# The RG-LRU gate products of a one-layer decoder step in float32r, with their low parts made on GpSimd

## The chip, the cores and the metric

The kernel runs on one core of one Trainium2 chip. A core has five engines that run at the same time, each with its own list of instructions: TensorE (PE in the profile, its weight loads PEld) multiplies matrices and writes to PSUM, VectorE (DVE) and ScalarE (ACT) work on tiles of 128 partitions, GpSimd (POOL) can do simple tile operations but reaches no PSUM, and SyncE (SP) only issues DMAs. An engine executes its list in order; semaphores make it wait for others. The metric is the device time of one execution in microseconds (us). Before the change it is 1437.67 us, the median of three runs (1437.34 to 1437.91).

## The reference

One layer of a decoder for a prompt of 256 tokens and 8 single-token samples, so 264 columns (N) that go through the same weights. The part that the change touches is the recurrent group (RG-LRU) at its beginning:

```python
  xn = rmsnorm(x, g_mix);  z = xn @ w_in
  xr, conv_new = causal_conv(z[..., OFF_RGX:OFF_RGG], conv_buf, conv_w, conv_b)
  r  = sigmoid(block_diag(xr, w_rg_a, b_rg_a))      # 8 blocks of 128 x 128
  ig = sigmoid(block_diag(xr, w_rg_x, b_rg_x))
  log_a = -RG_C * r * softplus(-lam);  a = exp(log_a)
  h  = scan(a, sqrt(1 - exp(2 * log_a)) * (ig * xr), h0)
```

Beside it in the same layer stands an mLSTM group, which also updates a matrix state C for each of the 8 samples and 4 heads, then come the output projection, attention to 256 memory tokens and a SwiGLU network. Everything is float32 in the reference.

## The kernel before

**Three passes.** In this kernel's trace four float32 products of 264 columns take TensorE 1.58 us, while one in float32r, a shorter form, follows the last after 0.11 us. The kernel therefore splits nearly every operand x into a high part h (x copied to float32r, on ScalarE) and a low part x - h (on VectorE), and `mm3` (L287) does three float32r matmuls: high by high, high by low, low by high. The right operand is taken in another column order (`turn`), so a result in PSUM is read back with `unturn` and written with `halves`. The gate products are an exception: `rg_gen` multiplies fp32 by fp32, one matmul for each of 8 chunks and 2 gates.

**Steps.** The weights come in steps of 128 x 2048 elements, listed in `steps`: four steps for the first quarter columns of w_in (0 to 3), four single ones (4 to 7) that finish the eight chunks of the recurrent input, step 8 for the mLSTM gates (`pe_if`), then q and k, v, the recurrent gate branch (from step 25), and so on. The main loop (L1489) goes through them. For step i it first hands out the evacuations of earlier steps, splits the weights of step i + 1 (`split_half`, two halves h0 and h1, with high priority; `st["split"]` and `st["low"]` remember the last high and low part), emits the matmuls of step i, loads the weights of step i + 3 on SP (`load_piece`, five buffers "raw"), and calls `pump`. The split weights lie in four buffers "w", so a half waits until TensorE is through with the one four halves earlier.

**Side work.** `pump` (L323) runs generators such as `rg_gen`, `ml_gates`, `ml_sample` up to a due time, by price formulas for VectorE and ScalarE (L65 to L96); a generator that yields STEP goes on at the next pump at the earliest. What the pump emits has only a place in the program. The tile framework's scheduler then orders the instructions of each engine itself, by priority and by its own simulated times, except on SP and where `in_order` or `manual_schedule` fixes the order of the program: ScalarE and VectorE up to step 3, TensorE up to step 6. `tc.issue_after(x)` puts an instruction behind x on x's engine.

**The first steps.** In steps 0 to 3 a piece of w_in holds four chunks, `load_first` (L209) sends each of the first six chunks (4 i + c < 6) as a DMA of its own, and the others two by two. SP's list (L1463 to L1475) takes turns between parts of x and chunks; behind piece 1 it sends `vecs[:, 16:]`, all vectors of the layer but the first gain.

**Recurrence.** `evac_rgx` brings a chunk from PSUM into a tile, `rg_conv` makes the convolution on VectorE, and `rg_gen` (started at step 7) loads the gate weights (`wrg`, two DMAs of 512 KB on SP), makes the coefficients (`rg_coef`), and after every second chunk emits four gate products and their sigmoids. The tiles come from the pool "B" with 26 buffers.

**Samples.** `ml_sample` (L859) goes through 4 heads and 8 samples: two ScalarE copies with a scale into t2, one VectorE update of C, two VectorE products with a sum; C goes out by DMA from GpSimd's queue.

Of the kernel before, what the change touches and what calls it, by code (L numbers as in the profile page):

```python
# [17 lines left out]
P = 128  # L18
# [77 lines left out]
def layer_kernel(ctx: ExitStack, tc, xT, memT, vec, wrg, w_in, w_out, w_q, w_k, w_v, w_o,  # L96
# [112 lines left out]
    def load_first(i, c):  # L209

        src = steps[i][0].rearrange("p (n c m) -> p n c m", c=4, m=P)
        if c % 2 == 0:
            raws.setdefault(i, []).append(B([P, 1024]))
        r = raws[i][c // 2].rearrange("p (n c m) -> p n c m", c=2, m=P)
        if 4 * i + c < 6:
            sp.dma_start(r[:, :, c % 2], src[:, :, c])
        elif c % 2:
            sp.dma_start(r, src[:, :, c - 1: c + 1])
# [307 lines left out]
                                 ts[:, :, 0:1], op0=OP.mult, op1=OP.add)  # L526

    def rg_gen():
        wr = [B([P, 8, P]), B([P, 8, P])]
        for j in range(2):  # L530
            sp.dma_start(wr[j], wrg[:, j * 8: j * 8 + 8, :])
        rg_coef()
        r, ig = Arr(RGB), Arr(RGB)
        for n in range(RGB):
            while rg["zn"] <= n:
                yield STEP
            rg_conv(n)
            yield 1.5
            if n % 2 == 0:
                continue  # L540
            yield STEP
            for q in (n - 1, n):
                for t, j, b in ((r, 0, "ba"), (ig, 1, "bx")):
                    ps = bank("ax")
                    pe.matmul(ps[:, :N], wr[j][:, q, :], rg["xr"](q), start=True, stop=True)
                    last = act.activation(t(q), ps[:, :N], AF.Sigmoid, bias=V(b, q))
            yield 0.1
        yield STEP
        xr, c = rg["xr"], rg["c"]
        e2 = Arr(RGB)  # L550

        for n in range(RGB):
            with tc.issue_after(last.ins), tc.issue_after(st["split"].ins):
                act.activation(e2(n), r(n), AF.Exp, scale=c[:, 8 + n: 9 + n])
                le = act.activation(r(n), r(n), AF.Exp, scale=c[:, n: n + 1])
                act.activation(e2(n), e2(n), AF.Relu, scale=-1.0, bias=ones[:, 0:1])
            dve.tensor_mul(ig(n), ig(n), xr(n))
            yield 0.8
        for n in range(RGB):
            with tc.issue_after(le.ins), tc.issue_after(st["split"].ins):  # L560
                act.activation(e2(n), e2(n), AF.Sqrt)
            dve.tensor_mul(ig(n), ig(n), e2(n))
            yield 0.4
        h = Arr(RGB)
        rg["h"] = h
        for n in range(RGB):
            dve.tensor_tensor_scan(h(n)[:, :T], r(n)[:, :T], ig(n)[:, :T], 0.0, op0=OP.mult, op1=OP.add)
            yield 0.6
        h0 = V("h0", 0, 64).rearrange("p (n b) -> p n b", b=NS)
        for q in range(2):  # L570
            hq, rq_, iq = (t.tile(q)[:, :, T:N] for t in (h, r, ig))
            dve.tensor_mul(hq, rq_, h0[:, 4 * q: 4 * q + 4, :])
            dve.tensor_add(hq, hq, iq)
            act.activation(hlast[:, 4 * q: 4 * q + 4, :], h.tile(q)[:, :, T - 1: N], AF.Copy)
        yield 0.3
# [52 lines left out]
    def evac_if(ps):  # L628
        R = Arr(7)
        ml["R"] = R  # L630
        for q in range(2):
            pool_e.memset(R.tile(q), 0.0)
        x, a = R(0)[0:36], R(1)[0:36]
        act.activation(gbias[0:4], V("bi")[0:4], AF.Copy)
        act.activation(gbias[32:36], V("bf")[0:4], AF.Copy)
        act.activation(halves(a), unturn(ps[64:100, :N]), AF.Copy)
        dve.tensor_add(halves(x), unturn(ps[0:36, :N]), halves(a))
        dve.tensor_mul(x, x, rstd[0:36, :])
        dve.tensor_scalar(x, x, gbias[0:36], None, op0=OP.add)
        ml["gates"] = side(ml_gates(), 0)  # L640
# [218 lines left out]
    def ml_sample():  # L859
        while not ml["gates"].done:  # L860
            yield STEP
        qk = ml["qk"]
        ks, qs = qk.tile(1)[:, :, T:N], qk.tile(0)[:, :, T:N]
        sc, Dg = bcs[:, :, 0:8], bcs[:, :, 8:16]

        def load(h, b4):
            C = B([P, 4, 2, P])
            pool_e.dma_start(C, c0T[h, :, b4 * 4: b4 * 4 + 4])
            return C

        loaded = [load(0, 0), load(0, 1)]
        x = ltmp(64)
        kd = ltmp(32).rearrange("p (h b) -> p h b", b=NS)
        by4 = lambda t: t.rearrange("p h (g b) -> p h g b", b=4)
        x4 = x.rearrange("p (h g j b) -> p h g j b", g=2, j=2, b=4)
        dve.tensor_mul(kd, ks, Dg)
        dve.tensor_copy(x4[:, :, :, 0], by4(kd))
        dve.tensor_copy(x4[:, :, :, 1], by4(qs))
        n0 = V("n0", 0, 32).rearrange("p (h b) -> p h b", b=NS)
        dve.tensor_mul(snew, n0, sc)  # L880
        dve.tensor_add(snew, snew, kd)
        dve.tensor_mul(ssum[:, 1], snew, qs)
        yield 0.6
        yield STEP
        ps = bank("ax")
        pe.transpose(ps[0:64, 128:256], x, ident)
        yield STEP
        rows = ltmp(128)
        act.activation(rows[0:64, :], ps[0:64, 128:256], AF.Copy)
        scr = drm.tile([64, P], F32, name="scr")  # L890
        pool_e.dma_start(scr, rows[0:64, :])
        yield 0.5
        def fetch(h, b4):
            C = loaded.pop(0) if loaded else load(h, b4)
            kq = B([P, 2, 4, P])
            r0 = (2 * h + b4) * NS
            src = scr[r0: r0 + NS, :].rearrange("b d -> (b d)")
            ml["fetch"] = pool_e.dma_start(kq.rearrange("p j b d -> p (j b d)"), src.partition_broadcast(P))
            return C, kq

        ahead = [fetch(0, 0), fetch(0, 1)]
        yield STEP
        for h in range(H):
            while ml.get("vn", 0) < 2 * h + 2 or "last" not in ml:
                yield STEP
            for b4 in range(2):
                C, kq = ahead.pop(0)
                n = 2 * h + b4 + 2
                for bb in range(4):
                    b = b4 * 4 + bb  # L910
                    t2 = sb.tile([P, 264], F32, tag="dw", bufs=2, name=nm("dw"))[:, 0: T]
                    t2 = t2.rearrange("p (v d) -> p v d", d=P)
                    with tc.issue_after(ml["exp"].ins):
                        for vb in range(2):
                            act.activation(t2[:, vb, :], kq[:, 0, bb, :], AF.Copy,
                                           scale=ml["v"](2 * h + vb)[:, T + b: T + b + 1])
                    with tc.issue_after(ml["last"].ins):
                        dve.scalar_tensor_tensor(C[:, bb], C[:, bb], sc[:, h, b: b + 1], t2,
                                                 op0=OP.mult, op1=OP.add)
                    j = sb.tile([P, 2, T], F32R, tag="ds", bufs=2, name=nm("ds"))[:, 0, 0: P].bitcast(F32)  # L920
                    for vb in range(2):
                        dve.scalar_tensor_tensor(j, C[:, bb, vb, :], 1.0, kq[:, 1, bb, :], op0=OP.mult,
                                                 op1=OP.mult, accum_out=nums[:, 2 * h + vb, b: b + 1])
                    yield 0.8
                if n < 2 * H:
                    ahead.append(fetch(n // 2, n % 2))
                with tc.issue_after(ml["fetch"].ins):
                    last = pool_e.dma_start(o_sc[h, :, b4 * 4: b4 * 4 + 4], C)
        while min(ml.get("pn", 0), ml.get("vtn", 0)) < H:
            yield STEP  # L930
        with tc.issue_after(last.ins):
            pool_e.dma_start(kept_k, ml["kb"])
            for q in range(2):
                ml["kept"] = pool_e.dma_start(kept_v[q], ml["vts"][q])
            pool_e.dma_start(o_h, hlast)
            pool_e.dma_start(o_cp, cpo)
            pool_e.dma_start(o_cs, cso)
            pool_e.dma_start(o_sn, snew)
        yield 0.1
# [529 lines left out]
    for i in range(1, 3):  # L1469
        for c in range(0, 4, 2):  # L1470
            load_x(sp, 4 * i + c, 4 * i + c + 2)
            load_first(i, c)
            load_first(i, c + 1)
        if i == 1:
            sp.dma_start(vecs[:, 16:], vec[:, 16:])  # L1475
    kept, early = ExitStack(), ExitStack()
    kept.enter_context(tc.manual_schedule(engines={mybir.EngineType.PE}))
    early.enter_context(in_order())
# [10 lines left out]
    for i, (src, cols, pef, evf, need) in enumerate(steps):  # L1489
# [41 lines left out]
        if i == 0:  # L1531
            for c in range(0, 4, 2):
                load_x(sp, 12 + c, 14 + c)
                load_first(3, c)
                load_first(3, c + 1)
        else:
            load_piece(i + LD)
        pump(pe.clock + SLACK)
        if i == 24:
            st["ng"] = side(ml_norm(), 6)  # L1540
# [122 lines left out]
```

## Time and profile before

| what | value |
|---|---|
| time, median of 3 runs | 1437.67 us |
| the profiled execution's own time | 1437.94 us |
| its span, first to last instruction | 1436.2 us |
| mean granted TensorE clock | 0.998 |
| PE ax<-B,B 128x264, the gate products | 32 records, mean 389 ns |
| PE mm<-B,w 128x264, float32r | 10448 records, mean 276 ns |
| DVE w<-raw,w 128x1024, a low part | 488, mean 1232 ns |
| ACT w<-raw 128x1024, a high part | 488, mean 1056 ns |
| POOL subtractions 128x256 | 32 in L1213 (mean 1143 ns), 16 in L1267 (mean 996 ns) |

A record's duration on TensorE is from its entry into the array to its modelled end; records overlap, so what a matmul costs is the distance from one start to the next. A timeline row reads: start, duration, engine, line, operation, output<-inputs, size, count, and in brackets the idle time before it with what ended it. A row of windows holds for each engine its busy time and count (PE, PEld, DVE, ACT, POOL), then the granted clock, the share of the DMA engines and GB/s. L61 is the line of a helper through which all PE, DVE and ACT instructions go, so groups are told apart by tiles.

### The profile page before, as it was taken

What the parts mean: (1) busy time and instruction counts of PE and PEld (TensorE: products, weight loads), DVE (VectorE), ACT (ScalarE), POOL (GpSimd) and SP (SyncE); (2) the same over time, 40 slices, a digit from 0 to 9 for tenths busy, and PEclk for the clock granted to TensorE, in tenths of its full rate; (3) what the DMA queues carried; (4) which work ended last, traced back from release to release, by engine and by line L of the source; (5) the groups of instructions that cost most, each with busy time, mean ns of one, the idle gap of its engine ahead of it and who ended that gap; (6) DMA issues with size and microseconds to landing.
All of it is one profiled execution on the core that took longest, in us unless ns stands there. A gap on an engine that the chain in (4) does not pass through costs nothing.

```text
span 1436.2 us, 29864 instructions
## 1 busy us (share of the span) xinstructions
PE 1423.6 (99%) x11959; PEld 1401.9 (98%) x11959; DVE 1039.2 (72%) x1974; ACT 802.7 (56%) x1291; POOL 125.1 (9%) x195
## 2 busy tenths in 40 slices
PE   9999999999999999999999999999999999999997
PEld 9999999999998999999999999999999999999997
DVE  7957898997899999977666655555656655566565
ACT  7778876775556666665554444334444433444474
POOL 0000220000224434300000000000000000000000
PEclk9999999999999999999999999999999999999999
DMA  8755897557899887846555555555555555555573
GB/s 301 232 195 179 303 360 294 186 194 252 289 347 388 295 335 273 322 161 214 192 192 200 195 192 200 197 191 195 201 192 193 200 195 192 198 196 194 164 242 127
DMA packets 98139, 329.16 MB, mean 229 GB/s; under 512 B 10864, under 2 KB 17440, under 8 KB 98000
## 3 DMA queue, kind: packets, MB, share of 16 engines
q1 hardware_dynamic: 81840, 271.96, 54.1%
q0 software_dynamic: 15296, 54.21, 10.2%
q8 instruction: 93, 1.52, 0.4%
q10 hardware_dynamic: 864, 1.08, 0.2%
q14 instruction: 46, 0.38, 0.1%
HBM read 314.36 MB, written 12.86 MB: 228 GB/s over the span
## 4 chain that ended last, share of the span: by engine, by line
PE 69%; DVE 1%; issue 0%; ACT 0%; POOL 0%; DVEq 0%; POOLq 0%; ACTq 0%
PE mm L61 67%; PE ax L61 2%; DVE B L61 0%; DVE w L61 0%; DVE dw L61 0%; POOL ds L1213 0%; DVE t L61 0%; ACT w L61 0%; ACT t L61 0%; DVE ax L61 0%; ACT dw L61 0%; ACT ds L61 0%; DVE rstd L61 0%; DVE osm L61 0%; DVEq L1640 0%
## 5 line engine op out<-in xcount | busy, mean ns | idle before, releaser
L61 PE MATMUL mm<-B,w 128*128 128x264 f32 (+1 forms) x10960 | 1280.9, 279 | 0.7 <-DVE w L61 0.7
L61 PEld LDWEIGHTS mm<-B,w 128*128 128x128 f32 x10960 | 1261.0, 189 | 8.3 <-DVE w L61 0.9
L61 DVE TENSOR_TENSOR w<-raw,w 128x1024 fp32r<-128x1024 f32 (+1 forms) x506 | 612.7, 1213 | 303.4 <-ACT w L61 302.5
L61 ACT ACTIVATE w<-raw 128x1024 fp32r<-128x1024 f32 (+1 forms) x506 | 525.2, 1041 | 500.2 <-PE mm L61 345.9
L61 PE MATMUL mm<-w,B 128*128 128x512 f32 x384 | 86.5, 380 | 0.0
L61 PEld LDWEIGHTS mm<-w,B 128*128 128x128 f32 x384 | 70.7, 189 | 9.4
L1554 POOL TENSOR_TENSOR B<-B,rstd 128x264 f32<-128x264 f32 x4 | 2.8, 743 | 801.9 <-ACT B L61 801.9
L61 DVE TENSOR_TENSOR t<-mm,rstd 128x264 f32<-128x264 f32 x96 | 41.5, 432 | 28.9 <-PE mm L61 28.8
L61 DVE SCALAR_TENSOR_TENSOR B<-B,dw 128x256 f32<-128x256 f32 x128 | 53.7, 471 | 2.8 <-ACT dw L61 2.6
L61 DVE TENSOR_TENSOR xres<-xres,mm 128x264 f32<-128x264 f32 (+1 forms) x81 | 34.1, 423 | 25.0 <-PE mm L61 25.0
L61 DVE SCALAR_TENSOR_TENSOR dw<-B,qsm,dw 128x256 f32<-128x256 f32 x96 | 47.9, 505 | 0.7
L1213 POOL TENSOR_TENSOR ds<-dw,ds 128x256 fp32r<-128x256 f32 x32 | 36.5, 1143 | 105.5 <-ACT ds L61 105.4
L61 PE MATMUL ax<-B,B 128*128 128x256 f32 (+3 forms) x276 | 43.7, 300 | 0.4 <-DMA B<-wrg 0.4
L61 PEld LDWEIGHTS ax<-B,B 128*128 128x128 f32 x276 | 37.7, 191 | 2.4 <-DMA B<-wrg 0.8
L61 ACT ACTIVATE B<-xres,vecs 128x264 fp32r<-128x264 f32 (+1 forms) x64 | 32.3, 504 | 10.4 <-DVE xres L61 8.6
L61 ACT ACT_TABLE_LOAD x21 | 26.9, 1283 | 4.1 <-issue 2.2
L1202 POOL DMA_DIRECT2D B<-kcT x32 | 17.3, 539 | 130.2 <-DVE B L61 117.0
L61 ACT ACTIVATE dw<-B,qsm 128x256 f32<-128x256 f32 x32 | 16.2, 506 | 19.7 <-issue 8.0
L61 ACT ACTIVATE t<-xres 128x264 f32<-128x264 f32 (+1 forms) x46 | 18.7, 408 | 14.0 <-DVE xres L61 13.8
L61 ACT ACTIVATE B<-t 128x264 fp32r<-128x264 f32 (+1 forms) x60 | 24.1, 408 | 1.8 <-DVE t L61 1.8
L61 ACT ACTIVATE dw<-ax,dw 128x256 f32<-128x256 f32 x32 | 15.0, 469 | 17.4 <-DVE dw L61 16.5
L61 ACT ACTIVATE ds<-dw 128x256 fp32r<-128x256 f32 x32 | 13.2, 414 | 19.7 <-DVE dw L61 19.6
(177 smaller groups left out, 695.9 us busy)
## 6 DMA issues: line engine op xcount, KB each, us to landing
raw<-w_gu SPq DMA_DIRECT2D x176, 512.0 KB, 3.6
raw<-w_d SPq DMA_DIRECT2D x80, 512.0 KB, 3.6
raw<-w_in SPq DMA_DIRECT2D x74, 512.0 KB, 5.2
raw<-w_out SPq DMA_DIRECT2D x32, 512.0 KB, 4.3
raw<-w_q SPq DMA_DIRECT2D x32, 512.0 KB, 4.8
B<-kcT POOLq DMA_DIRECT2D x32, 512.0 KB, 8.3
B<-vcT POOLq DMA_DIRECT2D x32, 512.0 KB, 9.7
raw<-w_k SPq DMA_DIRECT2D x32, 512.0 KB, 4.8
```

Of the source, the lines that this page charges most:

```text
L61: return f(*a, **k)
L1202: pool_e.dma_start(kc, kcT[h, b])
L1213: pool_e.tensor_sub(ws[:, 1], acc, ws[:, 0].bitcast(F32))
L1554: e.tensor_mul(st["y"](c), st["y"](c), r)
```

## The change

- `rg_gen` takes weights that were loaded earlier: their two DMAs are put on SP's list in step 3 of the main loop, behind the load of step 6's weights. It splits them (two tiles of 128 x 1024): high part on ScalarE, low part on GpSimd.
- After every second chunk it splits the two chunks of convolution output in the same way (128 x 528), and each gate product is an `mm3` of three float32r matmuls; the sigmoid reads PSUM through `unturn`.
- Chunks 2 and 3 of piece 1 come in a DMA each.
- `vecs[:, 16:]` is sent behind the last first chunk instead of behind piece 1.
- The two copies of the mLSTM gate biases on ScalarE are put behind the last weight split's high part.
- Each sample's update of C on VectorE is put behind the last weight split's low part, besides the one that it was behind.

```diff
-        if 4 * i + c < 6:
+        if 4 * i + c < 8:
             sp.dma_start(r[:, :, c % 2], src[:, :, c])
...
     def rg_gen():
-        wr = [B([P, 8, P]), B([P, 8, P])]
+        wr = rg["wr"]
+        rg_coef()
+        wr2 = []
         for j in range(2):
-            sp.dma_start(wr[j], wrg[:, j * 8: j * 8 + 8, :])
-        rg_coef()
+            wh, wl = B([P, 8, P], F32R), B([P, 8, P], F32R)
+            act.activation(wh, wr[j], AF.Copy)
+            pool_e.tensor_sub(wl, wr[j], wh.bitcast(F32))
+            wr2.append((wh, wl))
+            yield 1.1
...
+            x2, o = B([P, 2, 2, N], F32R), (n - 1) % 4
+            x = rg["xr"].tile(n // 4)[:, o: o + 2, :]
+            act.activation(x2[:, 0], x, AF.Copy)
+            pool_e.tensor_sub(x2[:, 1], x, x2[:, 0].bitcast(F32))
+            yield 0.6
             yield STEP
...
-                    pe.matmul(ps[:, :N], wr[j][:, q, :], rg["xr"](q), start=True, stop=True)
-                    last = act.activation(t(q), ps[:, :N], AF.Sigmoid, bias=V(b, q))
+                    mm3(ps[:, :N], tuple(w[:, q, :] for w in wr2[j]),
+                        (x2[:, 0, q - n + 1], x2[:, 1, q - n + 1]), True, True)
+                    last = act.activation(halves(t(q)), unturn(ps[:, :N]), AF.Sigmoid, bias=V(b, q))
...
-        act.activation(gbias[0:4], V("bi")[0:4], AF.Copy)
-        act.activation(gbias[32:36], V("bf")[0:4], AF.Copy)
+        with tc.issue_after(st["split"].ins):
+            act.activation(gbias[0:4], V("bi")[0:4], AF.Copy)
+            act.activation(gbias[32:36], V("bf")[0:4], AF.Copy)
...
-                    with tc.issue_after(ml["last"].ins):
+                    with tc.issue_after(ml["last"].ins), tc.issue_after(st["low"].ins):
                         dve.scalar_tensor_tensor(C[:, bb], C[:, bb], sc[:, h, b: b + 1], t2,
...
-        if i == 1:
-            sp.dma_start(vecs[:, 16:], vec[:, 16:])
...
+            sp.dma_start(vecs[:, 16:], vec[:, 16:])
         else:
             load_piece(i + LD)
+        if i == 3:
+            rg["wr"] = [B([P, 8, P]), B([P, 8, P])]
+            for j in range(2):
+                sp.dma_start(rg["wr"][j], wrg[:, j * 8: j * 8 + 8, :])
         pump(pe.clock + SLACK)
```

## The prediction

> **What bounds the kernel now.** I read the page's head first, then the chain that ended last, then who TensorE waited for.
>
> ```profile
> span 1436.2 us, 29864 instructions
> PE 1423.6 (99%) x11959; PEld 1401.9 (98%) x11959; DVE 1039.2 (72%) x1974; ACT 802.7 (56%) x1291; POOL 125.1 (9%) x195
> DVE  7957898997899999977666655555656655566565
> ```
>
> ```profile
> 715.32 707.41 PE mm L61 x6288
> ```
>
> ```profile
> PE mm L61 <- DVE w L61: 0.7, 1, 0.7
> PE ax L61 <- DMA B<-wrg: 0.4, 1, 0.4
> ```
>
> TensorE is busy for 99% of the span, and in its last long piece one matmul follows another every 707.41 / 6288 = 0.1125 us. What it waits for shows as two short waits in the middle. So the time can only fall by what TensorE executes or by such waits, and anything that makes a new wait costs in full. The second thing to see is VectorE's row of tenths: 9 in the second slice (36 to 72 us) and in the slices around 200 us. There the cover is thin, though the mean of 72% says otherwise.
>
> **The gate products.** These are the rows of TensorE's timeline for the second group (73 us) and for the first (54 us).
>
> ```profile
> 73.41 1.94 PE L61 MATMUL ax<-B,B 128*128 128x264 f32 x8
> 74.99 0.47 PE L61 MATMUL mm<-B,w 128*128 128x264 f32 x1
> ```
>
> ```profile
> 54.35 0.61 PE L61 MATMUL ax<-B,B 128*128 128x264 f32 x2
> 55.32 1.60 PE L61 MATMUL ax<-B,B 128*128 128x264 f32 x6 [0.36 <-DMA B<-wrg]
> 56.57 0.69 PE L61 MATMUL mm<-B,w 128*128 128x264 f32 x3
> ```
>
> Four fp32 products (two chunks, two gates) leave eight records and take 74.99 - 73.41 = 1.58 us. The first float32r matmul behind them lasts 0.47 instead of the 0.28 of the others, so 0.19 more: 1.77 us a group. The change makes twelve float32r matmuls of it, 12 x 0.1125 = 1.35. Four groups give 4 x 0.42 = **1.7 us less**. The group at 54 us takes 56.57 - 54.35 = 2.22, that is 0.64 over its 1.58: the late weights. Their DMA is now issued in step 3 of the main loop instead of step 7, so **0.6 us less**. What is late next is the split of these weights, below.
>
> **The first chunks.** This stage is fed by DMA.
>
> ```profile
> 7.83 1.27 SPq L1475 DMA_DIRECT2D vecs<-vec  x1
> 13.90 0.63 ACT L61 ACTIVATE w<-B 128x512 fp32r<-128x512 f32 x1 [0.92 <-DMA B<-w_in]
> 15.36 0.40 ACT L61 ACTIVATE gbias<-vecs 4x1 f32<-4x1 f32 x2
> 16.74 0.63 ACT L61 ACTIVATE w<-B 128x512 fp32r<-128x512 f32 x1 [0.44 <-DMA B<-w_in]
> ```
>
> ```profile
> 14.32 0.28 PE L61 MATMUL mm<-B,w 128*128 128x264 f32 x1
> 14.58 0.60 PE L61 MATMUL ax<-B,w 128*128 128x264 f32 x3
> ```
>
> ScalarE waits 0.92 us for chunks 2 and 3 of piece 1, which come in one DMA, and 0.44 for the next piece, behind the vectors whose issue alone holds SP for 1.27. The change sends the two chunks apart (one issue more on SP) and the vectors behind all first chunks. TensorE loses only 14.58 - 14.32 - 0.11 = 0.15 here, and its restart is 0.10 longer (0.60 against 0.50). I take the sum and a little for the next piece, **0.3 us less**; bounds 0 and 0.5. ScalarE and VectorE gain more, some 0.8 us (0.92 + 0.44 less what TensorE then asks for). The gate bias copies would wait for the vectors now; they go behind a split, and cost their 0.4 us there beside float32r matmuls. SP's later loads have the vectors ahead of them, but no more bytes in all: nothing.
>
> **The samples' state updates.** VectorE's and TensorE's timelines around the wait, and the windows.
>
> ```profile
> 195.21 1.04 ACT L61 ACTIVATE w<-raw 128x1024 fp32r<-128x1024 f32 x1
> ```
>
> ```profile
> 196.96 1.22 DVE L61 TENSOR_TENSOR w<-raw,w 128x1024 fp32r<-128x1024 f32 x1
> ```
>
> ```profile
> 196.33 1.18 PE L61 MATMUL mm<-B,w 128*128 128x264 f32 x9
> 198.23 2.97 PE L61 MATMUL mm<-B,w 128*128 128x264 f32 x24 [0.72 <-DVE w L61]
> ```
>
> ```profile
> 194.00:200.00 6.00, 5.28 (x47) 5.08 (x46) 6.00 (x28) 5.42 (x15) 0.53 (x1) 1.00 0.99 386
> ```
>
> Nine matmuls from 196.33 should end the series at 196.33 + 9 x 0.1125 = 197.34; the next comes at 198.23: 0.89 us. VectorE was never idle (6.00 of 6); it did sample updates while the low part, ready at 196.25, began at 196.96. With the new edge no update is put ahead of the newest low part. VectorE's total stays, so updates move back, into cover. ScalarE's high part also came late (195.21), which the edge doesn't order directly. Bounds 0 and 1.0; I take **0.85 us less**. The added wait queues VectorE's evacuations behind it for at most one low part, 1.22 us.
>
> **The new split, and its cover.** Added are two weight parts of 1024 columns and four input parts of 528, each a ScalarE copy and a GpSimd subtraction.
>
> ```profile
> 36.78 1.06 ACT L61 ACTIVATE w<-raw 128x1024 fp32r<-128x1024 f32 x1 [1.57 <-PE mm L61]
> 39.93 1.06 ACT L61 ACTIVATE w<-raw 128x1024 fp32r<-128x1024 f32 x1 [1.72 <-PE mm L61]
> ```
>
> ScalarE idles 1.57 and 1.72 us at 35 to 40 us, when the early weights have landed, and a copy is 1.06: nothing. GpSimd isn't the worry as an engine (9% busy) but as VectorE's neighbour:
>
> ```profile
> L1213 POOL TENSOR_TENSOR ds<-dw,ds x32: 726/1166/1743, 362.5 to 607.5; 128x256 fp32r<-128x256 f32 x32
> ```
>
> ```profile
> 401.97 0.74 POOL L1213 TENSOR_TENSOR ds<-dw,ds 128x256 fp32r<-128x256 f32 x1
> 402.31 1.50 DVE L61 TENSOR_TENSOR w<-raw,w 128x1024 fp32r<-128x1024 f32 x1 [0.57 <-ACT w L61]
> ```
>
> ```profile
> 588.95 0.41 DVE L61 TENSOR_TENSOR t<-t,mm 128x256 f32<-128x256 f32 x1
> 589.00 0.73 POOL L1213 TENSOR_TENSOR ds<-dw,ds 128x256 fp32r<-128x256 f32 x1 [2.93 <-ACT ds L61]
> ```
>
> A low part on VectorE that starts inside a GpSimd subtraction takes 1.50 instead of 1.22: 0.28 later for 256 columns. One with an operand in PSUM (t,mm) isn't slowed (0.41). For 1024 columns the block is between 4 x 0.28 = 1.1 and 4 x 0.74 = 3.0 us; VectorE is always waiting in this stage, so I take 2.0. [...]
>
> Now the stage in which they run.
>
> ```profile
> 28.00:40.00 12.00, 12.00 (x106) 11.85 (x105) 11.86 (x17) 8.37 (x17) 0.00 (x0) 1.00 0.66 209
> 40.00:47.00 7.00, 7.00 (x65) 7.00 (x64) 6.90 (x17) 6.42 (x25) 0.00 (x0) 1.00 0.77 253
> 47.00:54.00 7.00, 7.00 (x64) 7.00 (x64) 7.00 (x19) 6.22 (x13) 0.00 (x0) 1.00 0.87 276
> 54.00:62.00 8.00, 7.64 (x60) 7.03 (x59) 8.00 (x19) 6.18 (x12) 0.00 (x0) 1.00 0.71 235
> ```
>
> ```profile
> 41.09 0.43 DVE L61 TENSOR_TENSOR B<-mm,rstd 128x264 f32<-128x264 f32 x1
> 41.44 1.10 DVE L61 TENSOR_TENSOR B<-ax,rstd 128x264 f32<-128x264 f32 x3
> 42.45 0.76 DVE L61 TENSOR_TENSOR B<-mm,rstd 128x264 f32<-128x264 f32 x2
> 52.91 1.21 DVE L61 TENSOR_TENSOR w<-raw,w 128x1024 fp32r<-128x1024 f32 x1
> ```
>
> VectorE (third figure) is full from 28 to 62 us: 11.86 of 12, 6.90 of 7, 7.00 of 7, 8.00 of 8. Every block pushes all its later work back. The place where it decides is step 9: its first low part ends at 52.91 + 1.21 = 54.12, and at 54.35 TensorE, two matmuls into that step, turned to the gate group. Without that group there, the matmul that needs this low part would come at 54.35: **0.23 us of cover**. The group can't fill it any more, since its input's low part now comes behind the same VectorE work.
>
> Two blocks are 4.0 us. The six evacuations from 41.09 to 43.2 read PSUM and run on; the second subtraction falls about there, so I let 1.4 of the 4.0 go: 2.6 us late. VectorE comes 0.8 earlier and TensorE 0.3. The wait at step 9 is 2.6 - 0.8 + 0.3 - 0.23 = **1.9 us more**. Bounds: 0, where the blocks fall beside PSUM operands or after step 9; 2 x 3.0 - 0.73 = 5.3. The input parts, 528 columns (0.74 x 528 / 256 = 1.5 us each), come in and behind step 9 and cost nothing while step 10's cover lasts:
>
> ```profile
> 58.58 1.21 DVE L61 TENSOR_TENSOR w<-raw,w 128x1024 fp32r<-128x1024 f32 x1
> 61.71 0.61 PE L61 MATMUL mm<-B,w 128*128 128x264 f32 x4
> ```
>
> Both low parts of step 10 are done at 59.79, and step 10 begins near 62. [...]
>
> **The sum.** The profiled execution took 1437.94 us, the span and 1.74 around it; the median is 1437.67. Removed: 1.7 + 0.6 + 0.3 + 0.85 = 3.45. Added: 1.9. Net -1.55: 1436.4 against the profiled execution, and **1436.1** from the median, from which I count on.
>
> **Rivals.**
> - *The cover holds.* The weight parts run beside PSUM evacuations or behind step 9, or a 1024-column subtraction blocks little. For it: GpSimd is empty in all four windows above (0.00 in the fifth figure), so the parts can run at any time, and the planner may put low parts ahead of deferrable conv work. Against it: VectorE has no idle slot in these windows. All 3.45 come: 1434.2, range 1433.5 to 1434.8.
> - *The samples' edge does nothing,* since ScalarE's late high part was the cause, with the wait at step 9 as forecast: 1436.1 + 0.85 = 1436.95.
> - *Slower: GpSimd's long form.* The middle one of its 32 subtractions takes 1166 ns, which for 1024 columns makes 4.7 us each. Were all of it a block, VectorE is 9.3 late, the wait at step 9 is 9.3 - 0.73 = 8.6, and the time 1437.67 - 3.45 + 8.6 = 1442.8. It decides from the point at which the two block VectorE for more than 3.45 + 2.9 + 0.73 = 7.1 us together. Against it: that row's length holds GpSimd's own waiting for VectorE; undisturbed it is 726 ns.
>
> **How the numbers follow.** The forecast has 0.44 (its own range, for blocks from 2.1 to 4.2 us in sum: 1435.6 to 1437.7), the holding cover 0.38, the samples' edge without effect 0.10, slower 0.08. A measurement of this kernel can tell about 0.2%, 2.9 us, from no change: faster is below 1434.8, slower above 1440.5. Faster gets the cover's 0.38 and 0.02 of the forecast's edge, 0.40; slower 0.08; the rest 0.52. The range 1433.6 to 1438.3 leaves out the slow rival and the outer ends of the others.
>
> **What would show it.** The groups ax<-B,B at 128x264 should be twelve records in 1.35 us, with no 0.47 behind them. No wait for wrg. A wait for DVE w, or for a GpSimd low part, of 1.5 to 3.6 us near 54 us is the forecast; none there means that the cover held. VectorE's low parts between 36 and 50 us should show single ones of 2.5 to 4 us instead of 1.22 where a GpSimd subtraction lies beside them. Near 198 us the 0.72 wait should be gone. I am wrong if new waits come elsewhere, where the planner has ordered anew: in steps 17 to 22, or at SP, should a buffer of tag B be short while the four new weight tiles live.

## The result, and the profile after

The changed kernel takes 1442.23 us (median of 7 runs, 1441.56 to 1443.58) against 1437.84 for the kernel before on the same chip (7 runs): ratio 1.0034, 95% interval 1.0024 to 1.0044. It is slower by 4.4 us. The forecast was 1436.1 with a range up to 1438.3: wrong in sign and outside the range.

First the head of the page of the changed kernel, the last long piece of its chain, and the two longest waits of TensorE for an engine's tile (total, times, longest).

```profile
span 1440.5 us, 29936 instructions
```

```profile
720.04 707.41 PE mm L61 x6288
```

```profile
PE ax L61 <- DVE acc_x L61: 2.6, 1, 2.6
PE mm L61 <- DVE w L61: 2.1, 1, 2.1
```

The last half is the same to the hundredth (707.41 for 6288) and starts 4.72 later. Two single waits, 4.7 us together, are new. To see where they lie, I counted off TensorE's records of float32r matmuls with a weight tile, 48 to a step (32 in step 8), and took each step's first. Start minus that of the kernel before, in us; the rows below the first are the experiments that follow.

| kernel | step 4 | 6 | 9 | 12 | 17 | 32 | 48 |
|---|---|---|---|---|---|---|---|
| changed | -0.27 | +7.41 | +7.41 | +6.73 | +5.68 | +4.62 | +4.68 |
| e1 copy behind | +0.13 | -0.03 | +1.62 | +1.87 | +0.98 | -0.09 | -0.02 |
| e2 low on VectorE | +0.28 | +8.43 | +8.42 | +5.78 | +6.08 | +6.39 | +17.60 |
| e3 both | +0.07 | -0.09 | +0.33 | -0.81 | -0.52 | -0.20 | +12.38 |
| e4 edge alone | +0.20 | +0.04 | +0.04 | +0.40 | +0.40 | -0.59 | -0.52 |
| e5 as e3, not priced | -0.15 | -0.31 | -0.16 | -0.68 | -0.95 | -2.02 | -1.95 |
| e6 early fetch | -0.16 | +6.28 | +6.28 | +5.92 | +4.87 | +3.81 | +3.87 |
| e7 split later | -0.02 | -0.18 | -0.18 | +1.68 | +2.14 | +2.46 | +13.03 |
| e8 fp32 gates | +0.75 | +0.59 | +0.59 | -0.04 | -0.03 | -1.02 | -0.84 |
| e9 wait filled twice over | -0.84 | +8.32 | +8.32 | +7.96 | +6.90 | +5.85 | +5.91 |
| e10 low later | -0.80 | -0.92 | -0.92 | -3.61 | -2.09 | -3.15 | -3.09 |
| e11 wait filled | -0.75 | +3.81 | +3.81 | +3.51 | +2.46 | +1.47 | +1.66 |

The whole loss of the changed kernel falls into step 5 (-0.43 at its start, +7.41 at the next one's: 7.84 us). Behind it the change wins: 1.7 us from step 9 to 17 and 1.0 at step 32, though a new wait lies among these steps too (below). These are its timelines in step 5, ScalarE's, VectorE's, GpSimd's and TensorE's.

```profile
30.36 1.04 ACT L61 ACTIVATE w<-raw 128x1024 fp32r<-128x1024 f32 x1
34.58 1.06 ACT L61 ACTIVATE B<-B 128x1024 fp32r<-128x1024 f32 x1 [3.18 <-DMA B<-wrg]
35.54 1.04 ACT L61 ACTIVATE w<-raw 128x1024 fp32r<-128x1024 f32 x1
```

```profile
36.62 2.54 DVE L61 TENSOR_TENSOR w<-raw,w 128x1024 fp32r<-128x1024 f32 x1 [2.72 <-ACT w L61]
39.08 2.58 DVE L61 TENSOR_TENSOR B<-B 128x264 f32<-128x264 f32 x1
41.70 0.43 DVE L61 TENSOR_TENSOR acc_x<-acc_x,B 128x264 f32<-128x264 f32 x1
```

```profile
35.72 5.65 POOL L535 TENSOR_TENSOR B<-B,B 128x1024 fp32r<-128x1024 f32 x2 [22.34 <-DMA raw<-w_in]
```

```profile
36.63 0.49 PE L61 MATMUL mm<-B,w 128*128 128x264 f32 x2 [0.32 <-ACT w L61]
39.22 0.38 PE L61 MATMUL mm<-B,w 128*128 128x264 f32 x1 [2.09 <-DVE w L61]
42.18 1.25 PE L61 MATMUL ax<-acc_x,ones 128*128 128x264 f32 x2 [2.59 <-DVE acc_x L61]
```

Read them as a chain. The scheduler has put the copy of the first gate weights into ScalarE's list between the two high parts of step 5. ScalarE stands 3.18 us waiting for that copy's DMA, and step 5's second high part (35.54) stands behind it. VectorE waits 2.72 for that. Then its low part takes 2.54 instead of 1.22, and a sum of 264 columns 2.58 instead of 0.43, 3.5 us more in all, both beside GpSimd's two subtractions (35.72 to 41.37). The text calls this GpSimd's hold on VectorE. TensorE waits 0.32 + 2.09 + 2.59 = 5.0 us. And then it runs slowly; the window of 40 to 47 us (busy time and count of PE, PEld, DVE, ACT, POOL, then the granted clock):

```profile
40.00:47.00 7.00, 4.82 (x22) 4.61 (x23) 6.86 (x9) 0.85 (x2) 3.24 (x4) 0.54 0.55 178
```

22 matmuls took 4.82 us, 0.219 each, at a granted clock of 0.54. Two of them are fp32 products of the norm. In the kernel before, these two take 0.25 us from the first one's start (36.92) to the next matmul's (37.17), and with 0.19 for the changeover behind them and 20 x 0.1125 the same 22 make about 2.7 us: 2.1 us more. 5.0 + 2.1 is 7.1 of the 7.84. Three suspects therefore lie on top of each other: the wait for the DMA, GpSimd's hold on VectorE, and the clock.

### The profile page after: what moved, and what is told of

The parts are those of the page before. It is cut to its first block, busy times and chain, and to the rows that moved or that the text cites. A ratio compares the mean times of both kernels' runs of the same rounds, so it can differ in the third digit from the quotient of the medians.

```text
span 1440.5 us, 29936 instructions
## 1 busy us (share of the span) xinstructions
PE 1424.4 (99%) x11975; PEld 1403.4 (97%) x11975; DVE 1047.6 (73%) x1974; ACT 807.0 (56%) x1297; POOL 136.8 (9%) x201
## 4 chain that ended last, share of the span: by engine, by line
PE 69%; DVE 1%; issue 0%; ACT 0%; POOL 0%; DVEq 0%; POOLq 0%; ACTq 0%
PE mm L61 67%; PE ax L61 2%; DVE B L61 0%; DVE w L61 0%; DVE dw L61 0%; POOL ds L1225 0%; DVE t L61 0%; ACT w L61 0%; ACT t L61 0%; DVE ax L61 0%; ACT dw L61 0%; ACT ds L61 0%; DVE rstd L61 0%; DVE osm L61 0%; DVEq L1655 0%
## 5 line engine op out<-in xcount | busy, mean ns | idle before, releaser
L61 ACT ACTIVATE B<-B 128x264 f32<-128x264 f32 (+8 forms) x44 | 22.6, 529 | 6.9 <-DVE B L61 3.6
```

What stands on the lines that cost most here:

```text
L61: return f(*a, **k)
```

## The experiments

My theory was that the copy's place in ScalarE's list makes the loss, and GpSimd's hold on VectorE only lengthens it. The main rival was that the hold is enough by itself.

**e1, the copy behind step 5's parts.** To the changed kernel:

```diff
-            act.activation(wh, wr[j], AF.Copy)
+            with tc.issue_after(st["split"].ins):
+                act.activation(wh, wr[j], AF.Copy)
```

> The two ScalarE copies of the gate weights are put behind the high part of step 7's split; all else is the changed kernel. Order theory: the 7.8 us lost in step 5 start with the first copy, which waits for its DMA until 34.55 us in front of step 5's second high part; without it step 6 starts near 39.4 instead of 47.1 and the time is 1434 to 1435.5. Lock theory: the two 1024-column GpSimd subtractions block VectorE by 3.4 us wherever they run, so the loss only moves to steps 8 and 9: new waits for DVE w of 2 to 4 us near 50 to 56 us, 1436.5 to 1438.5.

Measured: 1437.17 us against 1437.65, ratio 0.9998 (0.9989 to 1.0007). The loss in step 5 is gone (-0.03 at step 6). New waits came at the start of step 8 and inside it, 1.65 us from step 6 to 9 by the table. So each theory had half of it: the order makes the loss in step 5, and the hold moves on to steps 8 and 9. VectorE's, GpSimd's and TensorE's timelines of e1:

```profile
43.41 0.76 DVE L61 TENSOR_TENSOR B<-mm,rstd 128x264 f32<-128x264 f32 x2
44.09 1.36 DVE L61 TENSOR_TENSOR w<-raw,w 128x1024 fp32r<-128x1024 f32 x1
45.37 2.32 DVE L61 SCALAR_TENSOR_TENSOR t<-vecs 128x8 f32<-128x8 f32 x1
```

```profile
41.99 5.68 POOL L536 TENSOR_TENSOR B<-B,B 128x1024 fp32r<-128x1024 f32 x2 [29.48 <-ACT B L61]
```

```profile
51.54 2.29 PE L61 MATMUL mm<-B,w 128*128 128x264 f32 x18 [0.88 <-DVE w L61]
54.07 2.07 PE L61 MATMUL mm<-B,w 128*128 128x264 f32 x16 [0.23 <-DVE w L61]
```

An operation of 8 columns took 2.32 us (0.15 in the kernel before) until GpSimd's second subtraction was over, while the evacuations from PSUM ran at their usual length (0.76 for two). Here the subtractions cost VectorE (1.36 - 1.21) + (2.32 - 0.15) = 2.3 us.

**e2, low parts on VectorE; e3, the same with e1's edit.** `dve.` adds the operation's price to VectorE's clock in the planner.

```diff
-            pool_e.tensor_sub(wl, wr[j], wh.bitcast(F32))
+            dve.tensor_sub(wl, wr[j], wh.bitcast(F32))
```

> The low parts of the gate weights on VectorE instead of GpSimd (two of 1.2 us each); ScalarE's order stays as in the changed kernel. Order theory: ScalarE still waits for the weights' DMA to 34.5 us, TensorE still loses 6 to 7.5 us in step 5, 1440.5 to 1442. Lock theory: the 3.4 us by which VectorE's instructions were stretched go, 1438 to 1439.

> Both edits: copies behind step 7's high part, and their low parts on VectorE. Order theory: 1434 to 1435.5, like the copies behind alone. Lock theory: better than the copies behind alone by 2 us or more. If VectorE's 2.4 us more of work find no cover, a wait for DVE w of 1 to 2 us at step 9 and 1435.5 to 1437.

Measured: e2 1454.79 (ratio 1.0120, 1.0106 to 1.0134), e3 1448.39 (1.0076, 1.0064 to 1.0089). In step 5 e2 loses 8.3 us with no GpSimd subtraction near, so the loss there doesn't need the hold. It isn't the wait for the DMA alone either: two low parts of the gate weights, 1.2 us each, now stand in VectorE's list, the first ahead of step 5's low part and the second ahead of the sum that TensorE waits for (ScalarE's, VectorE's and TensorE's timelines of e2):

```profile
36.35 1.06 ACT L61 ACTIVATE B<-B 128x1024 fp32r<-128x1024 f32 x1 [4.42 <-DMA B<-wrg]
```

```profile
37.44 1.23 DVE L61 TENSOR_TENSOR B<-B,B 128x1024 fp32r<-128x1024 f32 x1 [3.00 <-ACT B L61]
40.06 1.22 DVE L61 TENSOR_TENSOR B<-B,B 128x1024 fp32r<-128x1024 f32 x1
```

```profile
38.41 0.49 PE L61 MATMUL mm<-B,w 128*128 128x264 f32 x2 [1.54 <-ACT w L61]
39.85 0.38 PE L61 MATMUL mm<-B,w 128*128 128x264 f32 x1 [0.95 <-DVE w L61]
42.81 1.25 PE L61 MATMUL ax<-acc_x,ones 128*128 128x264 f32 x2 [2.58 <-DVE acc_x L61]
```

e3 has no loss there and only 0.42 at step 9. Both lose 11 to 13 us more at steps 42 to 44 (11.4 and 12.8 from step 41 to 48), which no expectation had. ScalarE's timeline of e3, and a wait of its TensorE:

```profile
267.92 0.42 ACT L61 ACTIVATE lt<-B 128x256 f32<-128x256 f32 x1 [8.68 <-DMA B<-memT]
```

```profile
PE mm L61 <- ACT B L61: 6.8, 1, 6.8
```

It is step 5's mistake in another place: an instruction that waits for a transfer stands in ScalarE's list in front of what TensorE needs. In the changed kernel the same instruction runs at 265.99 without a wait.

**e4, the samples' edge alone,** in the kernel before:

```diff
-                    with tc.issue_after(ml["last"].ins):
+                    with tc.issue_after(ml["last"].ins), tc.issue_after(st["low"].ins):
```

> The kernel before with one line of the change alone: the samples' updates of C behind the newest low part. If the 0.99 us that the changed kernel regains at step 31 is this edge's, the wait of 0.72 us for DVE w near 198 us is gone and the time is about 0.9 to 1.0 us under the kernel before; if it came from the shifted start of the kernel, nothing changes there.

Measured: 1437.22 against 1437.65, ratio 0.9998 (0.9988 to 1.0007). The median can't tell it, the trace can. This is TensorE's timeline of e4 where the kernel before had the wait of 0.72:

```profile
193.81 8.38 PE L61 MATMUL mm<-B,w 128*128 128x264 f32 x73
```

73 matmuls without a gap, and by the table the start of step 32 gains 0.99 on that of step 17.

**e5, as e3, but not priced.** The low parts go to VectorE and the planner's clock isn't told:

```diff
-            dve.tensor_sub(wl, wr[j], wh.bitcast(F32))
+            dve._engine.tensor_sub(wl, wr[j], wh.bitcast(F32))
```

> The high-part copies of the recurrence's weights stay behind step 5 as in e1, and their two low parts (1024 columns) go to VectorE, without being counted in the planner's own clock, so that the generators keep their places. Lock theory: what delayed steps 8 and 9 in e1 (1.05 and 0.6 us) was VectorE standing still beside GpSimd's two subtractions of 2.8 us (an 8-column operation took 2.32 us). On VectorE a low part of this size is 1.2 us, so the delay at steps 8 and 9 falls from 1.65 to at most 0.5 us, TensorE's step 12 comes at most 0.7 us after that of before (1.87 in e1), and the end at -1.2 us or lower: 1435.6 to 1436.6 us. Rival, VectorE has too much work there whichever engine does the split: the delay stays at 1.2 us or more, 1437.2 us or above.

Measured: 1435.13 against 1437.24, ratio 0.9986 (0.9978 to 0.9995): faster than both kernels. The two parts take 2.35 us, and at step 9 one wait is left (VectorE's and TensorE's timelines of e5):

```profile
44.75 2.35 DVE L536 TENSOR_TENSOR B<-B,B 128x1024 fp32r<-128x1024 f32 x2
```

```profile
55.15 3.25 PE L61 MATMUL mm<-B,w 128*128 128x264 f32 x26 [0.80 <-ACT w L61]
```

So e1's waits were GpSimd's hold and not a lack of time for the split. And e3's 12.8 us at step 42 hang on the price alone: the price is all that differs. The route from there to the late memT I infer from the lists' order, and tested no further; e7 below has the same wait with nothing priced, so the price is not the only way to it.

**e6, the weights fetched two steps earlier,** to the changed kernel:

```diff
-        if i == 3:
+        if i == 1:
             rg["wr"] = [B([P, 8, P]), B([P, 8, P])]
```

> The changed kernel with one edit: the weights of the gates are fetched behind step 1's work instead of step 3's; ScalarE's list keeps the copies where they are, one ahead of each of step 5's two high parts or so. Order theory (the loss is ScalarE's wait on the transfer, 3.18 us in front of step 5's high part, and then GpSimd's lock beside the late low part): with the data there, step 5's high parts come 1.06 us late each at most, and GpSimd's subtractions fall at 30 to 37 us; TensorE's step 6 comes 1.0 to 4.0 us after that of before, not 7.4, and the end at -1.5 to +1.5 us (1436.2 to 1439.5). Rival, the lock alone makes the loss, wherever the copies are: step 6 still 6 us or more late, 1441.5 or above. Second rival, the earlier transfers take the place of the steps' own weights: waits of TensorE on a DMA or on w at steps 2 to 4 that the kernel before doesn't have, of 1 us or more.

Measured: 1441.68, ratio 1.0031 (1.0018 to 1.0043), step 6 at +6.28: the rival's numbers. No wait for the DMA is left, and the loss is there. VectorE's, GpSimd's and TensorE's timelines of e6, and one of its windows:

```profile
32.15 2.49 DVE L61 TENSOR_TENSOR acc_x<-acc_x,B 128x264 f32<-128x264 f32 x1
34.56 2.86 DVE L61 TENSOR_TENSOR B<-B 128x528 f32<-128x528 f32 x1
37.35 1.21 DVE L61 TENSOR_TENSOR w<-raw,w 128x1024 fp32r<-128x1024 f32 x1
```

```profile
31.80 5.06 POOL L535 TENSOR_TENSOR B<-B,B 128x1024 fp32r<-128x1024 f32 x2 [18.31 <-ACT B L61]
```

```profile
38.62 4.75 PE L61 MATMUL mm<-B,w 128*128 128x264 f32 x25 [4.55 <-DVE w L61]
```

```profile
40.00:42.00 2.00, 2.00 (x11) 2.00 (x10) 2.00 (x4) 0.00 (x0) 0.00 (x0) 0.50 0.77 268
```

Two sums of the norm take 2.49 and 2.86 instead of the 0.43 and 0.70 of single ones in the kernel before (at 33.38 and 33.72): 4.2 us, and step 5's low part, queued behind them, begins at 37.35. My theory as stated falls: the loss needs no wait for the DMA. But the hold isn't alone here. In the kernel before, step 5's first low part stands ahead of these two sums (VectorE's timeline of before):

```profile
32.24 1.22 DVE L61 TENSOR_TENSOR w<-raw,w 128x1024 fp32r<-128x1024 f32 x1
33.38 0.43 DVE L61 TENSOR_TENSOR acc_x<-acc_x,B 128x264 f32<-128x264 f32 x1
```

In e6 the scheduler has put it behind them; no run has the hold there with the old order. What the changed kernel, e2 and e6 share is the place of the copies, ahead of step 5's second high part or of both. There the loss is 6 to 8 us with either delay or with both (the changed kernel), since the delays overlap; with the copies behind those parts, in e1, GpSimd's hold costs 1.65 by step 9.

**e7, the split behind step 9:** e1, with the generator waiting for the eighth chunk first.

```diff
         wr2 = []
+        while rg["zn"] <= 7:
+            yield STEP
```

> The split of the gates' weights is set behind step 9's work (the generator waits for the eighth projection, and the copies follow the last split issued); GpSimd still does the low parts. Lock theory: from step 9 on the weights of a step are split some 3 us and more ahead of need, so two blocks of 2 to 3 us of VectorE cost less than 0.5 us there; the gains of the gate products, the late weights and the samples' edge are left: step 12 at -0.5 to +0.5 us, the end at -1.5 to -3.0 us, 1434.7 to 1436.3 us. Rival, the block costs its full length wherever it lies: as e1, +1.5 us or more at step 12, 1437.2 or above. Second rival, the gates come later by a step and the recurrence's result is late at its consumers: a new wait of 1 us or more behind step 17.

Measured: 1450.85 (ratio 1.0096, 1.0082 to 1.0109), a miss. 10.6 of the 13.0 us (step 32 to 48) are again the memT wait at steps 42 to 44. The rest is at step 10, in VectorE's, GpSimd's and TensorE's timelines:

```profile
55.41 2.35 DVE L61 TENSOR_TENSOR c<-c 128x8 f32<-128x8 f32 x1
57.69 1.21 DVE L61 TENSOR_TENSOR w<-raw,w 128x1024 fp32r<-128x1024 f32 x1
58.82 4.17 DVE L61 TENSOR_SCALAR c<-c 128x8 f32<-128x8 f32 x1
61.07 2.67 DVE L61 SCALAR_TENSOR_TENSOR B<-B,vecs 128x256 f32<-128x256 f32 x9
```

```profile
54.09 7.04 POOL L538 TENSOR_TENSOR B<-B,B 128x1024 fp32r<-128x1024 f32 x2 [37.96 <-ACT B L61]
```

```profile
65.00 4.30 PE L61 MATMUL mm<-B,w 128*128 128x264 f32 x22 [2.57 <-DVE w L61]
```

Two operations of 8 columns, 0.15 us each elsewhere, hold VectorE too long, and the low part that TensorE waits for comes behind them. How long, the starts tell. Behind the first the next operation starts at 57.69, after 2.28 us. The record of the second runs for 4.17, but the next operation starts at 61.07, just when GpSimd's subtractions end (54.09 + 7.04 = 61.13), so VectorE stood for 2.25. That is 2.2 more for each than the 0.07 from one start to the next elsewhere (44.27 to 44.34 in the kernel before), 4.4 us in all. The two subtractions' price to VectorE was thus 2.3 (e1, beside PSUM evacuations), 3.5 (changed), 4.2 (e6) and 4.4 us (e7): it depends on what VectorE does beside them. Slow matmuls add their part here as well (mean granted clock 0.994 in e7's profiled execution, 0.998 before): from 65.00 the 22 matmuls take 4.1 us to the next record's start (69.10) where 22 x 0.1125 is 2.5.

**e8, fp32 gates kept:** the changed kernel without the split, and `pe.matmul` in fp32 as before.

> The changed kernel without the split: gate products in one fp32 pass as before, with the earlier fetch of their weights, the first chunks' order, the delayed biases and the samples' edge of the change. By the terms of the forecast: the wait on the late weights goes (-0.6 us at step 9 or 10), the first chunks give -0.3 us by step 4, the edge -0.85 to -1.0 us at step 32; end at -1.3 to -1.9 us, 1435.8 to 1436.4 us, with step 6 within 0.4 us of before. If the loss of the changed kernel had come from the fetch's place or the first chunks and not from the split, step 6 is 2 us or more late, and the time 1439 or above. If later steps give the gains back, the end lies within 0.5 us: 1437.2 or above.

Measured: 1436.46 against 1437.24, ratio 0.9992 (0.9984 to 1.0001). TensorE's timeline of e8 has the first gate group without a wait:

```profile
54.95 1.94 PE L61 MATMUL ax<-B,B 128*128 128x264 f32 x8
56.53 3.73 PE L61 MATMUL mm<-B,w 128*128 128x264 f32 x30
```

It takes 56.53 - 54.95 = 1.58, where before it was 2.22. From step 9 to 12 it wins 0.63, from 17 to 32 it wins 0.99. Its head is 0.75 late at step 4, though it is the changed kernel's head, and its end, -0.84 in the trace, misses the expected -1.3 to -1.9.

**e9 and e11, the clock.** e6 with extra matmuls of ones in front of step 5, into the bank that step 5 starts anew; 40 in e9, 20 in e11.

```diff
             w = W(i)
+            if i == 5:
+                for _ in range(20):
+                    pe._engine.matmul(ps[:, :P], ones, ones, start=True, stop=True)
```

> The kernel with the weights fetched behind step 1, and 40 extra matmuls of 128 columns of ones on TensorE ahead of step 5's first one, into the bank that step 5 then starts anew (some 40 x 0.11 us = 4.4 us of work by the rows of the kernel before); they add nothing to any output. There TensorE stood for 4.55 us waiting for the low part, then ran 15 matmuls at 0.220 us apart in place of 0.113, at a granted clock of 0.50. Theory: the slow matmuls are a second price of the wait itself, TensorE having stood idle; with the wait filled, all matmuls of step 5 come 0.113 us apart, the granted clock stays at 1.0, and step 6 comes 1.6 to 1.9 us earlier than without the filling: 4.4 to 4.7 us after that of before in place of 6.28; time 1439.6 to 1440.4 us. Rival: the lower clock belongs to that place or to the three engines' other work and not to TensorE's idleness: the 15 distances stay at 0.220 and step 6 comes 6.2 us late or more, 1441.4 us or above.

> As the run with 40 extra matmuls, which turned out as 80 records of 0.11 us, 9.1 us in all and 4.3 us more than the wait of 4.8 us, with 20 of them: 40 records, 4.5 us, about as long as the wait. Theory as there (the slow matmuls are the price of TensorE's idleness): all distances of step 5 behind the filling 0.113 us, granted clock 1.0, step 6 later than step 5 by 4.4 to 4.8 us more than in the kernel before (6.49 with the wait left empty), time 1439.4 to 1440.4 us. Rival (the slow matmuls only moved with the longer filling): distances of 0.220 us again, step 6 behind step 5 by 6 us or more over before, 1441.4 us or above.

Measured: e9 1443.85 (ratio 1.0043, 1.0030 to 1.0057), e11 1439.67 (1.0017, 1.0008 to 1.0027). I had mis-sized e9: each matmul left two records, so the filling took 9.1 us. TensorE's timelines, first of e9, then of e11, and a window of e11:

```profile
33.27 9.09 PE L1020 MATMUL mm<-ones 128*128 128x128 f32 x80
42.12 3.28 PE L61 MATMUL mm<-B,w 128*128 128x264 f32 x27
```

```profile
32.97 4.63 PE L1020 MATMUL mm<-ones 128*128 128x128 f32 x40
37.36 3.54 PE L61 MATMUL mm<-B,w 128*128 128x264 f32 x27
```

```profile
38.00:40.00 2.00, 2.00 (x19) 2.00 (x19) 2.00 (x4) 0.00 (x0) 0.00 (x0) 1.00 0.58 219
```

In both the clock stays at 1.0 behind the filling, 19 matmuls in 2 us where e6 had 11. From step 4 to 6 e11 loses 3.81 + 0.75 = 4.56 us against 6.28 + 0.16 = 6.44 in e6: 1.9 us less, and the time falls by 2.0, though TensorE executes more. So the slow matmuls are a second price of the wait.

**e10, the low parts two convolutions later,** to e5:

```diff
-            dve._engine.tensor_sub(wl, wr[j], wh.bitcast(F32))
...
+            if n == 1:
+                for j in range(2):
+                    dve._engine.tensor_sub(wr2[j][1], wr[j], wr2[j][0].bitcast(F32))
             yield 0.6
             yield STEP
```

> As the kernel with both low parts on VectorE, not counted in the planner's clock (1435.13 us), but the two low parts are issued behind the first two convolutions, so that VectorE's list has them after step 9's second low part in place of before step 8's. There TensorE waited 0.96 us for step 9's first low part and 0.54 us for a coefficient at 84.66 us, since VectorE was full from 40 to 56 us. Theory (the remaining loss is VectorE's 2.35 us in the wrong place): in the kernel before step 9's and 10's low parts are 2.5 to 5 us ahead of need; the wait of 0.96 us goes, step 10 comes 1.5 to 2.1 us earlier than in before, the end at -2.5 to -3.5 us, 1433.8 to 1434.8 us. Rival: the gate products now wait for the low parts, or step 10's low parts are late: a wait of 0.5 us or more at steps 9 to 11, and the end no better than -2.0 us, 1435.1 us or above.

Measured: 1435.33 against 1437.68, ratio 0.9983 (0.9974 to 0.9992). TensorE's timeline of e10 at step 9:

```profile
54.41 3.19 PE L61 MATMUL mm<-B,w 128*128 128x264 f32 x26 [0.23 <-ACT w L61]
```

The wait at step 9 falls from 0.80 to 0.23, a wait of 0.5 us for VectorE's c stays, and the trace ends at -3.09 where e5's ends at -1.95; of these 1.14 us between them, 0.65 are there at step 4 already. The medians of e5 and e10, on different chips, are 2.1 and 2.35 below their kernels before, and their intervals overlap; either beats both kernels of this study, and which of the two is better stays open.

## Why the prediction was wrong

- **What bounds the kernel:** right. TensorE's busy time is nearly the same (1424.4 us, 1423.6 before), and every new wait reached the end in full.
- **The gate products, 1.7 less:** right for each group. The rows of the changed kernel's second group, and its next matmuls:

```profile
80.38 1.51 PE L61 MATMUL ax<-B,B 128*128 128x264 f32 x12
81.73 1.51 PE L61 MATMUL mm<-B,w 128*128 128x264 f32 x12
```

  12 records in 81.73 - 80.38 = 1.35, and no longer first matmul behind them. Over the stage, from step 9 to 17, the changed kernel wins 1.73 where this term and the next make 2.3; see the input parts below.
- **The late weights, 0.6 less:** right, 0.64 in e8 (2.22 - 1.58).
- **The first chunks, 0.3 less:** not told apart. Step 4 starts between -0.84 and +0.75 in profiles of kernels that share this head; the scatter of the first loads is larger than the term. ScalarE's two waits weren't removed but moved: 0.39 (at 13.32) and 1.06 (at 16.47) in the changed kernel in place of 0.92 and 0.44.
- **The samples' edge, 0.85 less:** right, 0.99 in the changed kernel, e4 and e8 alike.
- **The new split's copies: "ScalarE idles 1.57 and 1.72 us at 35 to 40 us ... nothing".** This step failed. I placed the copies into gaps of the old order, with the weights landed. The scheduler placed the first one ahead of step 5's second high part, 3.18 us before its weights had landed, and the other right behind that part. The price was not 0: with the hold and the lower clock that followed from the place, step 5 lost 7.84 us, and with the copies behind step 5's parts (e1) this loss was gone. With it went the place that I had taken for GpSimd's subtractions. The prediction had named a new order as what would make it wrong, but looked for it in steps 17 to 22 and at SP.
- **GpSimd's hold, 4.0 us of which 2.6 reach the low parts, and 1.9 at step 9:** right in size. With the copies put by hand near where I had assumed them (e1) VectorE lost 2.3, and step 9 came 1.65 later; elsewhere the two blocks cost 3.5 to 4.4. Its length shows best at operations of 8 columns, which held VectorE for 2.32 us (e1), 2.28 and 2.25 us (e7). That evacuations from PSUM run on, as the forecast assumed, held in e1: two took 0.76 us beside a subtraction (at 43.41), as in the kernel before (at 42.45).
- **The input parts, "cost nothing while step 10's cover lasts":** this failed too, on a smaller scale. GpSimd's, VectorE's and TensorE's timelines of the changed kernel:

```profile
58.57 1.58 POOL L549 TENSOR_TENSOR B<-B,B 128x528 fp32r<-128x528 f32 x1 [15.33 <-ACT B L61]
```

```profile
59.01 2.22 DVE L61 TENSOR_TENSOR w<-raw,w 128x1024 fp32r<-128x1024 f32 x1
69.92 4.46 DVE L61 SCALAR_TENSOR_TENSOR B<-B,vecs 128x256 f32<-128x256 f32 x8
```

```profile
74.80 0.80 PE L61 MATMUL ax<-ident,B 128*128 128x4 f32 x6 [0.38 <-DVE c L61]
```

  A low part takes 2.22 instead of 1.21 beside the first, and eight operations that take 2.22 in the kernel before (63.50) take 4.46 beside the next two (GpSimd's, at 70.28 and 72.95). Behind them TensorE has a new wait of 0.38 us in step 11. That the hold made this wait is read from the order and was not tested apart. In e1 this stage wins only 0.64 of the 2.3, with 0.50 lost in the same place (at 70.50) and further waits in step 9, and so e1 ends at -0.02 in the trace and not at the forecast's -1.55, although its copies stand near where the forecast had them.
- **The rival on the slower side, 1442.8 at 0.08,** came near the time for another reason: it needed more than 7.1 us of block near step 9, and the two subtractions were 5.65 us long, in step 5.
- **What the forecast had no term for:** TensorE's lower granted clock behind a wait, 1.9 us in e6 (0.50 from 40 to 42 us) and about 2.1 in the changed kernel (0.54 from 40 to 47 us).

The savings were there: with the split kept out of the way (e5, e10) the kernel gains 2.0 to 3.1 us in the trace, of the 3.45 that the forecast counted as saved; the waits that are left at step 9 and for c take some of the rest.

## What to carry to other kernels

Where a scheduler orders the engines' lists, a new instruction doesn't go into the old trace's gaps: ask ahead of which high-priority work it may be put, and what it waits for there, above all a DMA; an edge behind that work (e1) is worth more than an earlier fetch (e6). Before work is moved to GpSimd because it is empty, look at what VectorE does in that stage: with no idle slot there, 2.35 us for two low parts on VectorE itself (e5) were cheaper than 5.68 us for them beside it (e1). Behind TensorE's waits of 2.57 us (e7), 4.55 us (e6) and 5.0 us in three pieces (changed), its slow matmuls took 1.6, 1.9 and 2.1 us on top; a forecast of such a wait has to have a term for them.

## What the runs showed of the hardware

- After TensorE had waited 4.55 us (e6), it ran 15 matmuls 0.220 us apart instead of 0.113, and its 25 matmuls from 38.62 to 43.20 took 4.58 us where 25 x 0.1125 is 2.8. The granted clock was 0.67 from 38 to 40 us, 0.50 from 40 to 42 and 0.98 from 42 to 44. In the changed kernel, with waits of 2.09 and 2.59 us, it was 0.50 from 40 to 46 us and 0.90 from 46 to 48. With e6's wait filled by useless matmuls (e11) it was 1.00 in each window from 30 to 46 us, and the 27 matmuls behind the filling took 3.37 us (37.36 to 40.73) where 27 x 0.1125 is 3.0.
- Shorter waits differ. Behind one of 2.57 us (e7, at 65.00) 22 matmuls took 4.1 us, and behind two of 1.15 and 0.77 us in a row (e7) 22 took 4.25 us (263.21 to 267.46), where 22 x 0.1125 is 2.5. In the window with the wait of 0.72 us in the kernel before (194 to 200 us) the granted clock was 1.00. From what length on a wait is followed by slow matmuls, these runs don't show.
- Two GpSimd subtractions of 1024 columns took 5.06 (e6) to 7.04 us (e7) a pair. Beside them VectorE's two sums in e6 took 2.1 and 2.2 us more (2.49 - 0.43, 2.86 - 0.70), and its two operations of 8 columns in e7 kept it 2.2 us longer each (2.28 and 2.25 to the next start, 0.07 elsewhere). Beside one of 528 columns a low part took 1.0 us more (2.22 - 1.21, the changed kernel at 59.01).
- None of GpSimd's instructions, 195 in the kernel before and 201 in the changed one, has an operand in PSUM (mm, ax); whether one could, no run shows.
